# Four small edits to a decoder layer: weight sums on VectorE in one group, ScalarE's copy before VectorE's sum, two orders

## The chip, the cores and the metric

One core of a Trainium2 chip runs the whole kernel. The metric is device time in microseconds, the median of several executions. The engines are TensorE (PE, with PEld for its weight loads), VectorE (DVE), ScalarE (ACT), GpSimd (POOL) and SyncE (SP), whose queue issues nearly all loads.

## What is computed

One decoder layer on 16 + 256 positions, width 2048, in float32:

```python
u = rms_norm(h, ffn1_norm_g);  h = h + 0.5 * swiglu(u, w_gate, w_up, w_down)     # first FFN, 5632 wide
u = rms_norm(h, mix_norm_g);   z = u @ w_in                                      # q, k, v, index heads, conv, two gates
y_attn = dsa_sparse_attention(q, k, v, qi, ki, wi, 64) @ w_attn_branch
y_conv = (gate_b * causal_depthwise_conv(gate_c * xc)) @ w_conv_branch
h = h + (sigmoid(ga) * y_attn + sigmoid(gc) * y_conv) @ w_out
u = rms_norm(h, ffn2_norm_g);  h = h + 0.5 * swiglu(u, w2_gate, w2_up, w2_down)  # second FFN
return h[:, 16:]
```

## The kernel before, in words

**Two numbers for one.** The matmuls run in a format with fewer bits than float32. Each weight tile and each activation is therefore split in two: ScalarE copies it into `hi` (`whi`, L215), VectorE subtracts that from the original to get `lo` (`wlo`, L216). A product takes three matmuls: hi x hi, hi x lo, lo x hi.

**One stream of weights.** `Stream` takes all weights in the order in which they are used. `load` (L167) issues the DMA of a 1 MB chunk on SP into a few rotating `raw` buffers; it waits there until the buffer's last reader is done. `split` makes whi and wlo of one piece (128 x 1024 at most) some pieces ahead of TensorE: `ahead` is 3 at first, with four buffers, and 5 with six from `widen` on, which comes before the second FFN. `next` hands one piece to TensorE; each call first splits ahead, then emits the work that was put off with `later` or `early`. That fixes the order of the instructions on every engine: the schedule is by hand, and each engine runs its queue in that order.

**Seven products for eight.** The gates and the second FFN work on 2 x 2 blocks of weights. A pair of kind C is multiplied plainly, in 8 products of 3 matmuls. The kinds S and D use 7 products (`group`), of sums of weights (`sa`, `sb`) and sums of tokens. For S, VectorE makes `sa` (L187) from the loaded chunk, then `sb` in two steps (L193, L194). For D, the DMA makes `sa`, under the name `sd`: one load on SP (L156), then an accumulating load of another part on POOL's queue (L157); the raw chunk holds the other three parts. `add_up` keeps up to three `sd` buffers ahead: two pairs are issued in `widen`, the others as earlier pairs are split. VectorE makes `sb` in both kinds, ahead of the split of the piece before the pair.

**Sums of tokens** (`sums_of_tokens`) are made per pair of features: ScalarE scales two tiles, VectorE makes three differences and sums (L617 to L619), and the result is split (L421, L422). The last argument of the function, `at`, puts it off by that many pieces.

**The output projection.** For the 16 tiles `po[d]`, the first six get 12 of their 16 blocks early and the last four later; the others run one after the other, in two pieces of 8 blocks. A bank holds the product with hi in its first and that with lo in its second half of columns. `add_to` (L411) adds both to h; `next_act2` and `square` follow a piece later and prepare the next norm.

**The second FFN.** Eleven groups of 512 features (`up_group`), then the down projection over 4, 4 and 3 of them (`down_group`), each in two halves. In group 0, `hook` puts the norm's matmuls (L1265) and the transposes of h (L1275, copied to `ht` by L1276) between the pairs. The norm's matmuls need the sum `ssq` (L1283), a VectorE step put off by one piece. After the last pair of kind D or S, `recombine` (L669 to L674) makes four tiles from the seven products' banks; `after_seven` and `after_end` add them to the result.

Of the kernel before, what the change touches and what calls it, by code (L numbers as in the profile page):

```python
# [9 lines left out]
F32 = mybir.dt.float32  # L10
F32R = mybir.dt.float32r
AF = mybir.ActivationFunctionType
ALU = mybir.AluOpType
AX = mybir.AxisListType

P = 128
# [35 lines left out]
WIDE = 512  # L52
NG = FF // WIDE
PAIRS = KD // 2
KINDS = "DCDCDCCC"
ORDER = [3, 0, 5, 1, 7, 2, 4, 6]
# [7 lines left out]


def pairs_up(g):
    return list(zip("CCCDCDCC", range(PAIRS)) if g == 0 else zip(KINDS, ORDER))


def pairs_gate(c):  # L70
# [3 lines left out]
def pairs_down(gs, half):  # L74
    a = list(gs)
    if len(a) > 3:
        kinds, at = [
            ("CCDCDCDC", [(0, 2), (1, 2), (0, 0), (2, 2), (1, 0), (3, 0), (2, 0), (3, 2)]),
            ("CDCDCDCC", [(0, 2), (0, 0), (1, 2), (1, 0), (2, 2), (2, 0), (3, 0), (3, 2)]),
        ][half]  # L80
    else:
        kinds, at = [
            ("CCDCDC", [(0, 2), (1, 2), (0, 0), (2, 0), (1, 0), (2, 2)]),
            ("CDDCCC", [(0, 2), (0, 0), (1, 0), (1, 2), (2, 0), (2, 2)]),
        ][half]
    return [(k, a[i], f) for k, (i, f) in zip(kinds, at)]

# [8 lines left out]
class Stream:  # L96
# [7 lines left out]
    def __init__(self, nc, raw_pool, split_pool):  # L104
        self.nc = nc
        self.raw_pools, self.raw_bufs, self.n_raw = [raw_pool], RAW_BUFS, 0
        self.split_pools, self.ahead, self.n_tiles = [split_pool], AHEAD, 0
        self.sum_pool = None
        self.loads, self.subs = [], []
        self.raw, self.ready, self.sums, self.summed = {}, {}, {}, set()  # L110
        self.n_loaded = self.n_split = self.at = 0
        self.blocks, self.waiting, self.steps = [], [], []
        self.first = []
        self.added, self.doubles, self.n_added = {}, [], 0
# [56 lines left out]
    def sum_ahead(self):  # L171

        add = self.nc.vector.tensor_add
        for g, kind, _, _, _ in self.subs[self.n_split : self.n_split + 2]:
            if kind == "sa" and self.sum_pool and g not in self.summed:
                self.load(g + self.raw_bufs)
                self.summed.add(g)
                raw = self.raw[g]
                sb = self.sum_pool.tile([P, 2 * WIDE], F32, name="sb", tag="sb")
                if g in self.added:  # L180
                    sa, one, last = self.sums[g, "sa"], raw[:, :WIDE], raw[:, 2 * WIDE : 3 * WIDE]
                else:
                    sa, one, last = (
                        self.sum_pool.tile([P, 2 * WIDE], F32, name="sa", tag="sa"),
                        raw[:, WIDE : 2 * WIDE], raw[:, 3 * WIDE :],
                    )
                    add(  # L187
                        sa.rearrange("p (q c) -> p q c", q=2),
                        raw[:, WIDE : 3 * WIDE].rearrange("p (q c) -> p q c", q=2),
                        raw[:, :WIDE].rearrange("p (q c) -> p q c", q=1).to_broadcast([P, 2, WIDE]),  # L190
                    )
                    self.sums[g, "sa"] = sa
                add(sb[:, :WIDE], sa[:, WIDE:], one)  # L193
                add(sb[:, WIDE:], sb[:, :WIDE], last)  # L194
                self.sums[g, "sb"] = sb
# [75 lines left out]
def tile_decoder_layer(  # L271
# [22 lines left out]
    nc = tc.nc  # L294
# [10 lines left out]
    st = Stream(nc, raw_pool, split_pool)  # L305
# [105 lines left out]
    def add_to(x, ps, scale, pairs):  # L411

        n = x.shape[1]
        nc.vector.scalar_tensor_tensor(x, ps[:, :n], scale, x, op0=ALU.mult, op1=ALU.add)
        if pairs:
            u = tmp.tile([P, T], F32, name="u", tag="sq")[:, :SEQ]
            nc.scalar.activation(u, ps[:, SEQ:], AF.Copy, scale=scale)
            nc.vector.tensor_add(x, x, u)

    def split_into(hi, lo, src):  # L420
# [200 lines left out]
    def sums_of_tokens(i, gain, to, at=0):  # L621

        x = small_tile("m0").rearrange("p (j t) -> p j t", j=2)
        t = small_tile("m1")

        def scaled(j):
            d = 2 * i + j
            nc.scalar.activation(x[:, j, :], h[:, d, META:], AF.Copy, scale=gain[:, d : d + 1])

        st.later(lambda: [scaled(j) for j in range(2)], at + 1)  # L630
        st.later(lambda: sums_into(t, x), at + 2)
        st.later(lambda: split_into(to[:, 0, :], to[:, 1, :], t), at + 3)
# [15 lines left out]

            st.later(after)

    def group(todo, hook, after_seven, after_end):

        kinds = [k for k, _, _ in todo]
        nc_ = kinds.count("C")
        ns = len(kinds) - nc_
        last = max(n for n, k in enumerate(kinds) if k != "C")
        q = {}

        def of(tag):
            if tag not in q:  # L660
                q[tag] = [bank(tag, tag), 0, {"q2": ns + 2 * nc_, "q3": ns + 2 * nc_, "q4": ns + 2 * nc_, "q8": 2 * nc_}.get(tag, ns)]
            return q[tag]

        buf = {}

        def recombine():
            a, v, x, e = (small_tile(n) for n in "avxe")
            buf.update(q2=a, q3=v, q4=x, q8=e)
            nc.scalar.activation(a, q["q1"][0], AF.Copy)  # L669
            st.later(lambda: nc.vector.tensor_sub(v, q["q6"][0], a), 1)  # L670
            st.later(lambda: nc.vector.tensor_add(x, q["q7"][0], v), 2)
            st.later(lambda: nc.vector.tensor_sub(v, q["q5"][0], v), 3)
            st.later(
                lambda: nc.vector.scalar_tensor_tensor(e, q["q5"][0], -1.0, x, op0=ALU.mult, op1=ALU.add), 4  # L674
            )
            if after_seven:
                for i, tag in enumerate(buf):
                    st.later(lambda tag=tag: after_seven(tag, buf[tag]), 5 + i // 2)

        for n, (kind, four, ts) in enumerate(todo):  # L680
            b11, b12, b21, b22 = four()
            if kind != "C":
                t1, t3, t2, t4 = (both(ts()[:, :, f * P : (f + 1) * P]) for f in range(4))
                for tag, t in (
                    ("q7", t3), ("q5", t1), ("q6", t2), ("q3", b22), ("q1", b11), ("q4", t4), ("q2", b21)
                ):
                    mac3(of(tag), t, st.next())
                if n == last:
                    st.early(recombine)
            else:  # L690
                plain_half(b11, b12, b21, b22, of("q2"), of("q3"))
                if n == len(todo) - 1:
                    st.early(lambda: after_end(q, buf, ("q2", "q3")))
                hook(n)
                plain_half(b11, b12, b21, b22, of("q4"), of("q8"))
        st.early(lambda: after_end(q, buf, ("q4", "q8")))

    with ExitStack() as mix:
# [37 lines left out]
        steps = st.steps  # L736
# [388 lines left out]

        act1 = act[:, :, :, LATER + META : LATER + T]
        made1 = {i: gp.tile([P, 2, 4 * P], F32R, name=f"made{i}") for i in SEVEN}
        for n, (i, to) in enumerate(made1.items()):
            sums_of_tokens(i, gains[1], to, 3 * n)

        ms, merged = {}, []
        places = [[("tA", 4)], [("tB", 4)], [("zz0", 2), ("zz1", 2)], [("c0", 4)]]
# [92 lines left out]
    room[0] = left  # L1225

    ht = [left.tile([P, D], F32, name=f"ht{j}") for j in range(NT)]
    more = left.tile([P, 3, 2, 4 * P], F32R, name="more")
    third = left.tile([P, 2, 4 * P], F32R, name="third")
    made_of(SEVEN[2], 12)  # L1230
# [89 lines left out]
    def down_group(gs, final):  # L1320
        for half in range(2):
            pairs = pairs_down(gs, half)

            def place(tag, half=half):
                j, c = PLACES[tag]
                c = half * 2 * WIDE + c * WIDE
                return j, c, ht[j][:, c : c + WIDE]

            met = dict.fromkeys(PLACES, 0)

            def add_half(tag, x, place=place, met=met):
                j, c, to = place(tag)
                nc.vector.scalar_tensor_tensor(to, x, 0.5, to, op0=ALU.mult, op1=ALU.add)
                met[tag] += 1
                if final and met[tag] == 2:
                    nc.sync.dma_start(out[j * P : (j + 1) * P, c : c + WIDE], to)

            def after_end(q, buf, tags, add_half=add_half):
                for tag in tags:
                    add_half(tag, q[tag][0])  # L1340

            group(
                [
                    (k, lambda g=g, f=f: four_of(mids[g], f, f + 1), lambda g=g, f=f: made_mid[g, f])
                    for k, g, f in pairs
                ],
                lambda n: n == 1 and half == 0 and turn_mid(("q6", "q1")), add_half, after_end,
            )

    right = []  # L1350
# [155 lines left out]
```

## Time and profile before

| | |
|---|---|
| median of 3 runs | 2152.8 us (2152.34 to 2153.24) |
| the profiled execution | 2151.74 us, its span 2150.0 us |
| busy | PE 2127.5 us (99%), DVE 1500.8 (70%), ACT 1081.8 (50%), POOL 82.3 (4%) |
| granted TensorE clock over the span | 0.999 |
| loads of kind D's sums | 48 on SP and 48 on POOL, 512 KB each |

Times in rows are microseconds from the start of the span. A row of a timeline gives start, duration, engine, line, operation, output<-inputs, and in brackets the idle time just before it with what ended it. L12 is line 12 of the kernel. Rows of waits read: engine, tile and line that waited, for whom, us in total, times, longest. The span ends with the output's DMAs; between the span and the execution's time lie 1.74 us.

### The profile page before, as it was taken

How to read it: one execution, taken by the hardware profiler on the slowest of the kernel's cores; microseconds unless marked ns; L12 is line 12 of the kernel's file. 1: busy time of each engine (PE TensorE's matmuls, PEld its weight loads, DVE VectorE, ACT ScalarE, POOL GpSimd, SP SyncE). 2: the span in 40 equal slices, each digit the busy share in tenths (PEclk: the TensorE clock that was granted, in tenths of full speed). 3: DMA queues.
4: the chain of work that ended last, by engine and by line, in shares of the span. 5: the costliest groups of instructions: out<-in, count | busy, mean ns of one | idle time of the engine just before them, and what ended most of it. 6: DMA issues, size and time to landing. Idle time of an engine off the chain costs nothing.

```text
span 2150.0 us, 32021 instructions
## 1 busy us (share of the span) xinstructions
PE 2127.5 (99%) x13045; PEld 1917.2 (89%) x13045; DVE 1500.8 (70%) x1919; ACT 1081.8 (50%) x1398; POOL 82.3 (4%) x94
## 2 busy tenths in 40 slices
PE   8999999999999999999999999999999999999999
PEld 8999999999999998889988888887888888888887
DVE  7555544455555556687578777678888988888887
ACT  6444433344444445465455555466555555555553
POOL 2000000000000000000000000010000000000000
PEclk9999999999999999999999999999999999999999
DMA  6555555555555555444555556469887887788773
GB/s 242 196 177 177 177 177 177 179 178 178 181 180 181 179 177 177 157 156 139 176 180 199 178 188 214 158 219 277 260 270 220 258 278 250 249 246 284 241 245 128
DMA packets 70996, 435.47 MB, mean 203 GB/s; under 512 B 7904, under 2 KB 8032, under 8 KB 30272
## 3 DMA queue, kind: packets, MB, share of 16 engines
q1 hardware_dynamic: 63648, 407.66, 53.6%
q0 software_dynamic: 7056, 25.59, 6.8%
q8 instruction: 102, 1.67, 0.3%
q14 instruction: 46, 0.38, 0.0%
q10 hardware_dynamic: 144, 0.17, 0.0%
HBM read 431.29 MB, written 2.10 MB: 202 GB/s over the span
## 4 chain that ended last, share of the span: by engine, by line
PE 92%; DVE 4%; ACT 1%; DMA 1%; issue 1%; POOL 1%; SPq 0%; ACTq 0%; POOLq 0%
PE q L593 13%; PE q L592 13%; PE q L594 13%; PE pd L388 4%; PE pd L386 4%; PE pd L387 4%; PE pg L387 4%; PE pu L387 4%; PE pg L388 4%; PE pu L388 4%; PE pg L386 4%; PE pu L386 4%; DVE wlo L216 2%; PE pbr L592 1%; PE pbr L594 1%; PE pbr L593 1%
## 5 line engine op out<-in xcount | busy, mean ns | idle before, releaser
L216 DVE TENSOR_TENSOR wlo<-raw,whi 128x1024 fp32r<-128x1024 f32 (+1 forms) x753 | 878.0, 1173 | 586.2 <-ACT whi L215 572.1
L215 ACT ACTIVATE whi<-raw 128x1024 fp32r<-128x1024 f32 (+1 forms) x753 | 760.2, 1016 | 876.1 <-PE q L594 219.2
L592 PE MATMUL q<-whi,act 128*128 128x512 f32 x833 | 325.7, 391 | 0.0
L593 PE MATMUL q<-wlo,act 128*128 128x512 f32 x833 | 324.7, 390 | 0.8 <-DVE wlo L216 0.8
L594 PE MATMUL q<-whi,act 128*128 128x512 f32 x833 | 324.3, 389 | 0.0
L386 PE MATMUL pd<-mid,whi 128*128 128x272 f32 x704 | 201.7, 286 | 0.0
L387 PE MATMUL pd<-mid,whi 128*128 128x272 f32 x704 | 201.7, 286 | 0.0
L388 PE MATMUL pd<-mid,wlo 128*128 128x272 f32 x704 | 201.7, 286 | 0.0
L386 PE MATMUL pg<-act,whi 128*128 128x272 f32 x672 | 192.7, 287 | 0.0
L387 PE MATMUL pg<-act,whi 128*128 128x272 f32 x672 | 192.5, 287 | 0.0
L388 PE MATMUL pg<-act,wlo 128*128 128x272 f32 x672 | 192.5, 287 | 0.0
L386 PE MATMUL pu<-act,whi 128*128 128x272 f32 x672 | 192.5, 286 | 0.0
L387 PE MATMUL pu<-act,whi 128*128 128x272 f32 x672 | 192.5, 286 | 0.0
L388 PE MATMUL pu<-act,wlo 128*128 128x272 f32 x672 | 192.5, 286 | 0.0
L593 PEld LDWEIGHTS q<-wlo,act 128*128 128x128 f32 x833 | 156.6, 188 | 33.6 <-DVE wlo L216 1.9
L594 PEld LDWEIGHTS q<-whi,act 128*128 128x128 f32 x833 | 156.5, 188 | 32.5
L592 PEld LDWEIGHTS q<-whi,act 128*128 128x128 f32 x833 | 156.7, 188 | 32.1
L386 PEld LDWEIGHTS pd<-mid,whi 128*128 128x128 f32 x704 | 132.6, 188 | 0.0
L387 PEld LDWEIGHTS pd<-mid,whi 128*128 128x128 f32 x704 | 132.6, 188 | 0.0
L388 PEld LDWEIGHTS pd<-mid,wlo 128*128 128x128 f32 x704 | 132.6, 188 | 0.0
L388 PEld LDWEIGHTS pg<-act,wlo 128*128 128x128 f32 x672 | 126.6, 188 | 0.0
L386 PEld LDWEIGHTS pg<-act,whi 128*128 128x128 f32 x672 | 126.6, 188 | 0.0
(288 smaller groups left out, 3787.0 us busy)
## 6 DMA issues: line engine op xcount, KB each, us to landing
raw<-in_wgu_dram SPq DMA_DIRECT2D x87, 1024.0 KB, 4.8
raw<-in_w_dram SPq DMA_DIRECT2D x84, 1024.0 KB, 6.0
raw<-in_wd_dram SPq DMA_DIRECT2D x44, 1024.0 KB, 4.7
raw<-in_w2d_dram SPq DMA_DIRECT2D x48, 768.0 KB, 6.3
raw<-in_wg_dram SPq DMA_DIRECT2D x32, 1024.0 KB, 4.8
raw<-in_wcv_dram SPq DMA_DIRECT2D x24, 1024.0 KB, 4.8
sd<-in_w2d_dram SPq DMA_DIRECT2D x48, 512.0 KB, 6.0
sd<-in_w2d_dram POOLq DMA_DIRECT2D x48, 512.0 KB, 7.7
```

The source lines that it names most:

```text
L215: nc.scalar.activation(to[0], raw, AF.Copy)
L216: nc.vector.tensor_sub(to[1], raw, to[0].bitcast(F32))
L386: nc.tensor.matmul(ps, whi, xhi, start=first, stop=False)
L387: nc.tensor.matmul(ps, whi, xlo, start=False, stop=False)
L388: nc.tensor.matmul(ps, wlo, xhi, start=False, stop=last)
L592: nc.tensor.matmul(ps, xhi, whi, start=n == 0, stop=False)
L593: nc.tensor.matmul(ps, xhi, wlo, start=False, stop=False)
L594: nc.tensor.matmul(ps, xlo, whi, start=False, stop=n == total - 1)
```

## The change

Four edits. In group 0 of the second FFN's up projection the pairs 3 and 5 are of kind S instead of D; the tile for their `sa` is lent by the second half of `ht[1]`. In `add_to`, ScalarE's copy of the second half is issued ahead of VectorE's sum. In the second half of the last down projection the kinds run C D C D C C instead of C D D C C C, and its recombination runs at once instead of spread over several pieces. In the gates, the third sums of tokens are put off by 16 pieces instead of 6.

```diff
 def pairs_up(g):
-    return list(zip("CCCDCDCC", range(PAIRS)) if g == 0 else zip(KINDS, ORDER))
+    return list(zip("CCCSCSCC", range(PAIRS)) if g == 0 else zip(KINDS, ORDER))
...
-            ("CDDCCC", [(0, 2), (0, 0), (1, 0), (1, 2), (2, 0), (2, 2)]),
+            ("CDCDCC", [(0, 2), (0, 0), (1, 2), (1, 0), (2, 0), (2, 2)]),
...
-        self.sum_pool = None
+        self.sum_pool = self.lent = None
...
-                        self.sum_pool.tile([P, 2 * WIDE], F32, name="sa", tag="sa"),
+                        self.lent if self.lent is not None else self.sum_pool.tile([P, 2 * WIDE], F32, name="sa", tag="sa"),
...
     def add_to(x, ps, scale, pairs):
         n = x.shape[1]
-        nc.vector.scalar_tensor_tensor(x, ps[:, :n], scale, x, op0=ALU.mult, op1=ALU.add)
         if pairs:
             u = tmp.tile([P, T], F32, name="u", tag="sq")[:, :SEQ]
             nc.scalar.activation(u, ps[:, SEQ:], AF.Copy, scale=scale)
+        nc.vector.scalar_tensor_tensor(x, ps[:, :n], scale, x, op0=ALU.mult, op1=ALU.add)
+        if pairs:
             nc.vector.tensor_add(x, x, u)
...
-    def group(todo, hook, after_seven, after_end):
+    def group(todo, hook, after_seven, after_end, spread=True):
...
+            for i, fn in enumerate(steps):           # steps: the four VectorE steps of recombine
+                st.later(fn, 1 + i if spread else 1)
             if after_seven:
                 for i, tag in enumerate(buf):
-                    st.later(lambda tag=tag: after_seven(tag, buf[tag]), 5 + i // 2)
+                    st.later(lambda tag=tag: after_seven(tag, buf[tag]), 5 + i // 2 if spread else 2)
...
-        for n, (i, to) in enumerate(made1.items()):
-            sums_of_tokens(i, gains[1], to, 3 * n)
+        for at, (i, to) in zip((0, 3, 16), made1.items()):
+            sums_of_tokens(i, gains[1], to, at)
...
     ht = [left.tile([P, D], F32, name=f"ht{j}") for j in range(NT)]
+    st.lent = ht[1][:, 2 * WIDE :]
...
                 lambda n: n == 1 and half == 0 and turn_mid(("q6", "q1")), add_half, after_end,
+                not (final and half == 1),
```

More of the change, by code (lines that the diff above doesn't have):

```diff
@@ L669, in recombine @@
             nc.scalar.activation(a, q["q1"][0], AF.Copy)
[L670 to L675, printed above, removed]
+            steps = [
+                lambda: nc.vector.tensor_sub(v, q["q6"][0], a),
+                lambda: nc.vector.tensor_add(x, q["q7"][0], v),
+                lambda: nc.vector.tensor_sub(v, q["q5"][0], v),
+                lambda: nc.vector.scalar_tensor_tensor(e, q["q5"][0], -1.0, x, op0=ALU.mult, op1=ALU.add),
+            ]
+            for i, fn in enumerate(steps):
+                st.later(fn, 1 + i if spread else 1)
             if after_seven:
                 for i, tag in enumerate(buf):
-                    st.later(lambda tag=tag: after_seven(tag, buf[tag]), 5 + i // 2)
+                    st.later(lambda tag=tag: after_seven(tag, buf[tag]), 5 + i // 2 if spread else 2)
         for n, (kind, four, ts) in enumerate(todo):
```

## The prediction

> **What bounds the kernel now.** I read the busy shares first, then TensorE's waits, then the chain of waits, then the timeline around each wait. TensorE is busy 99% of the span, so only its idle places can be won. Its waits over the whole run name them (engine, tile and line, for whom, us in total, times, longest):
>
> ```profile
> PE norm L1265 <- DVE ssq L1283: 4.3, 1, 4.3
> PE po L401 <- ACT whi L215: 2.7, 4, 0.8
> ...
> PE q L592 <- DVE ve L674: 1.1, 1, 1.1
> ```
>
> The longest stands early in the second FFN's group 0. The chain of waits (start, us, what) says what it waits for:
>
> ```profile
> 1439.86 5.13 DMA sd<-in_w2d_dram
> 1445.06 0.51 issue
> 1445.57 8.08 DMA sd<-in_w2d_dram
> 1453.68 0.70 DVE sb L193
> 1454.40 0.69 DVE sb L194
> 1455.09 2.27 DVE wlo L216 x2
> 1457.76 0.89 PE norm L1265 x4
> 1458.64 1.81 PE pht L1275 x8
> 1486.82 1.44 PE pht L1275 x12
> ```
>
> Two DMAs one after the other (a load, then an accumulating load on POOL's queue) make the first weight sum. VectorE stands before it with `sb`, and the small add `ssq` (L1283), which the norm's matmuls need, is queued behind. The windows show more (stretch, us, then busy time and count of PE, PEld, DVE, ACT, POOL, granted clock, DMA share, GB/s):
>
> ```profile
> 1457.80:1461.40 3.60, 3.60 (x15) 3.41 (x16) 3.60 (x4) 3.58 (x5) 0.00 (x0) 0.53 0.92 375
> 1461.40:1486.40 25.00, 25.00 (x111) 20.66 (x111) 19.61 (x29) 15.40 (x21) 2.62 (x3) 1.00 1.00 294
> ```
>
> After the stop TensorE runs at a granted clock of 0.53 for some 3.6 us, then at full clock with 25.00 / 111 = 0.225 us per matmul (0.227 is the spacing of the starts below). So I price a stop by start times, not by idle time:
>
> ```profile
> 1453.06 0.39 PE L594 MATMUL q<-whi,act 128*128 128x512 f32 x1
> ...
> 1461.45 0.39 PE L592 MATMUL q<-whi,act 128*128 128x512 f32 x1
> ```
>
> Between these starts lie 8.39 us. At full clock I expect 4 matmuls of 512 columns (0.91), 8 transposes (1.44 x 8/12 = 0.96) and the 4 norm matmuls (their 0.89 at half clock, so an estimate of 0.4): 2.27. The stop costs 6.1 us. [...]
>
> The second place is the start of the one-by-one output tiles of the output projection, in TensorE's timeline:
>
> ```profile
> 1378.63 2.04 PE L401 MATMUL po<-ms,whi 128*128 128x512 f32 x8
> ...
> 1396.41 2.00 PE L401 MATMUL po<-ms,whi 128*128 128x512 f32 x8
> ```
>
> Five half tiles (8 blocks each) take 17.78 us. Unhindered:
>
> ```profile
> 1396.40:1438.30 41.90, 41.90 (x242) 36.88 (x241) 33.50 (x53) 26.74 (x46) 4.03 (x4) 1.00 0.58 201
> ```
>
> 15 half tiles in 41.90 us, 2.79 each. So this place loses 17.78 - 13.97 = 3.8 us.
>
> **The change part by part.**
>
> *ScalarE's copy first.* At a tile's end VectorE multiplies one half of the bank into h (L414), ScalarE copies the other half (L417), VectorE adds it (L418). On each engine the order stays; what turns is who waits, as the waits of this stage show:
>
> ```profile
> ACT u L417 <- DVE h L414: 27.1, 16, 2.0
> ...
> DVE h L418 <- ACT u L417: 8.0, 16, 0.5
> ```
>
> All 16 tiles: ScalarE stands 1.7 us, with the next weight split (whi, L215) queued behind the copy, and VectorE 0.5 us; then VectorE stands again for that whi. With the copy first, ScalarE needs only the matmuls, done several us earlier, and copies while VectorE is still in its previous wlo. VectorE then runs L414 and L418 back to back. It saves 8.0 us of standing on VectorE over 16 tiles, and about as much again behind whi. Followed step by step at the place of the loss, each whi is then ready about 1 us before TensorE needs it. Bounds: 0, if the wait turns without getting shorter, to 3.8. I take 3.6, near the upper end, because VectorE is busy only 33.50 of 41.90 us even in the crowded part. From there on the stage is bound by TensorE. [...]
>
> *Group 0 with weight sums on VectorE.* Two pairs change from D to S. Removed per pair: a 512 KB load on SP, an accumulating 512 KB load on POOL, and 768 KB of raw; added: 1024 KB of raw on SP, in the same place of its queue, and one 128x1024 sum on VectorE. Traffic falls by 2 x 768 KB. The sum's row stands in the gates' first group, in the chain:
>
> ```profile
> 1105.38 1.23 DVE wlo L216
> 1107.60 1.15 DVE sa L187
> ```
>
> 2 x 1.15 = 2.3 us more on VectorE. The first lies where VectorE stands waiting for the DMA until 1453.68, the second in group 0 behind TensorE's pace, so both cost nothing; without that cover they would cost 2.3. VectorE's last work before it stood still:
>
> ```profile
> 1446.45 2.36 DVE L216 TENSOR_TENSOR wlo<-raw,whi 128x1024 fp32r<-128x1024 f32 x2 [0.44 <-ACT whi L215]
> ```
>
> With nothing but this change VectorE would begin the sum there, at 1448.8, and do sum, sb, sb, wlo, wlo, ssq (1.15 + 0.70 + 0.69 + 2.27 + 0.4, the last from 1457.36 to 1457.76): 1454.0 against 1453.3, when TensorE is ready. That leaves 0.8 idle and saves 5.3. With the faster output projection VectorE is some 4 us earlier relative to TensorE, and the stop goes: 6.1. Next in line is then the raw load of the second S pair. Its predecessor, 768 KB, took:
>
> ```profile
> raw<-in_w2d_dram SPq DMA_DIRECT2D x1, 768.0 KB, 9.8
> ```
>
> By size that is 13.1 us for 1024 KB. By the order of the queues its sum is wanted some 13 us after its issue, and TensorE can wait for it about 5 us more (both estimates from the paces above): hidden. The sum's tile is the half of ht[1] that the transposes fill only at the group's end; the second sum reuses it after the first's two reads, long done. The sd buffers are loaded as early as before, now for group 1; the third pair there has its load issued only when the first is split (last rival).
>
> *Third token sums later.* Their three VectorE steps fill the gap between the two rows above (1106.61 to 1107.60, 1.0 us), ahead of the second S pair's sum, which holds up the next wlo. TensorE there:
>
> ```profile
> 1110.19 0.39 PE L592 MATMUL q<-whi,act 128*128 128x512 f32 x1
> 1111.37 0.50 PE L593 MATMUL q<-wlo,act 128*128 128x512 f32 x1 [0.80 <-DVE wlo L216]
> 1111.71 0.40 PE L594 MATMUL q<-whi,act 128*128 128x512 f32 x1
> 1111.94 0.40 PE L592 MATMUL q<-whi,act 128*128 128x512 f32 x1
> ```
>
> 1.75 us for three matmuls instead of 0.68: 1.07 lost. Taking 1.0 us out ahead of it brings the wlo to its time with 0.1 to spare; I take 1.0 (0.8 to 1.07). The sums now stand ten blocks later, among plain pairs, where TensorE needs 12 x 0.227 = 2.7 us per split and VectorE about 1.2 plus one or two steps of 0.7; their 1.0 and the 0.7 of their split fit. They are first used in the next column of gates.
>
> *Order of the last half.* C D D C C C becomes C D C D C C. The second D's two sb steps stand today ahead of the step `ve`, which frees the bank that the first D's second matmul group writes:
>
> ```profile
> 2116.18 0.61 DVE sb L193
> 2116.81 0.69 DVE sb L194
> ```
>
> ```profile
> 2118.57 0.39 PE L592 MATMUL q<-whi,more 128*128 128x512 f32 x1
> ...
> 2121.30 0.39 PE L592 MATMUL q<-whi,more 128*128 128x512 f32 x1
> ```
>
> 2.73 us for six matmuls instead of 1.36: 1.37 lost. The sb steps (1.3) move behind `ve`, so I take 1.3 (0.9 to 1.37). In exchange the last recombination has two C pairs left (2 x 24 x 0.227 = 10.9 us) instead of three. It is 8 VectorE steps of about 0.65 and a copy of 0.6, 5.8 in all, and the change lets them run at once: hidden, and the tail behind the last matmul stays. If VectorE came to them over 5 us late, they would cost up to 5.
>
> **Sum.** 3.6 + 6.1 + 1.0 + 1.3 = 12.0 us. The profiled execution took 2151.74 (span 2150.0, 1.74 around it), 1.06 below the median. So 2139.7 for it, and 2152.8 - 12.0 = 2140.8 for the median.
>
> **The rivals.**
>
> *The wait turns and stays.* VectorE stands 0.5 us for the copy at each tile as now. Against it: ScalarE waits 1.7 us there for nothing else, so it can be early. The 3.8 stay and 0.8 of the norm's stop: 5.3 + 1.0 + 1.3 = 7.6 to 7.7, time 2145.1. Chance 0.08.
>
> *The raw loads bound the start of the one-by-one tiles.* The tiles before them are small and quickly used up, so three loads of 1024 KB come close together. If half the 3.8 stays: 2142.6. Chance 0.12.
>
> *A new wait in group 0*, on the second S pair's raw or on the lent tile. A stop of 4 us in place of 6.1, so 8.0 saved in all: 2144.8. Chance 0.08.
>
> *Slower: the third pair of group 1.* Its load and accumulation are issued when the group's first pair is split. Needed one D (21 matmuls), one C (24), one D and half a C later, 78 x 0.227 = 17.7 us, and VectorE leads TensorE there by some 4.6 us (an estimate from the same pace): 22.3. The slowest of this region:
>
> ```profile
> sd<-in_w2d_dram SPq DMA_DIRECT2D x1, 512.0 KB, 7.9
> sd<-in_w2d_dram POOLq DMA_DIRECT2D x1, 512.0 KB, 10.7
> ```
>
> With the 0.5 of issue between them, as in the chain, 19.1, so it is hidden by 3. It becomes slower than before from 22.3 + 12.0 = 34.3 us on; at 37 it would be 2155.5. Chance 0.03.
>
> **How the numbers follow.** The forecast has 0.67, with an own range of 2139.6 to 2142.0; a further 0.02 is for no change at all. The range 2139.6 to 2145.3 takes in the three rivals that are also faster. Faster by over 0.2% (4.3 us, about what a measurement of this kernel can tell): 0.94; the rest 0.03 and 0.03.
>
> **What would show it.** Right: no wait of TensorE for ssq, none for whi at the first one-by-one tiles, none at the gates' second S pair or at the last half's first D; ScalarE no longer waits for L414, VectorE's L414 hardly for the copy; clock 1.00 throughout group 0; 46 sd loads. Wrong: VectorE idle ahead of L414 in every tile; a wait for raw or sd in groups 0 and 1; VectorE still recombining at the last matmul.

## The result, and the profile after

The changed kernel takes 2140.69 us (median of 6 runs, 2140.57 to 2141.47); the kernel before, run beside it, 2152.66 (6 runs, 2152.18 to 2153.66). The ratio is 0.9945, its 95% interval 0.9932 to 0.9957. The forecast was 2140.8.

The profiled execution took 2141.47 us, its span is 2139.7. The busy shares and the loads of kind D's sums (groups of DMA issues: count, KB each, median us from issue to landing):

```profile
PE 2124.4 (99%) x13045; PEld 1915.1 (90%) x13045; DVE 1502.4 (70%) x1921; ACT 1083.5 (51%) x1398; POOL 79.2 (4%) x92
...
sd<-in_w2d_dram POOLq DMA_DIRECT2D x46, 512.0 KB, 8.2
```

TensorE executes as many matmuls as before. VectorE has two instructions more, POOL two fewer. The shares hardly differ; what has gone is in TensorE's waits over the whole run (engine, tile and line, for whom, us in total, times, longest):

```profile
PE start L386 <- ACT whi L215: 7.3, 2, 6.8
...
PE pbr L593 <- DVE ve L675: 0.4, 1, 0.4
```

The four waits that the prediction went for (norm on `ssq`, po on `whi`, q on `ve`, q on `wlo`) are gone. Behind the start of the run one is new: `pbr`, the product of the attention and convolution branches, waits for `ve`.

The sum of what went is best seen between TensorE's first and last matmul, first in the kernel before, then in the changed one (timeline):

```profile
6.01 0.59 PE L386 MATMUL start<-act,whi 128*128 128x272 f32 x1 [6.01 <-ACT whi L215]
...
2145.57 0.39 PE L594 MATMUL q<-whi,mid 128*128 128x512 f32 x1
```

```profile
6.76 0.60 PE L386 MATMUL start<-act,whi 128*128 128x272 f32 x1 [6.76 <-ACT whi L215]
...
2134.80 0.39 PE L595 MATMUL q<-whi,mid 128*128 128x512 f32 x1
```

2139.56 us has become 2128.04: 11.5 us less. The two profiled executions differ by 2151.74 - 2141.47 = 10.3 only. Of the rest, 0.75 us lie at the start, where the first weights came later in the second, and 0.5 us behind the last matmul: from its start to the end of the span it is 4.4 us before and 4.9 after, and 4.9 too in experiments 2 and 3, which leave the last half alone.

**The output projection** (timeline of TensorE; the same five half tiles as in the prediction):

```profile
1379.11 2.11 PE L401 MATMUL po<-ms,whi 128*128 128x512 f32 x8
...
1393.18 1.09 PE L401 MATMUL po<-ms,whi 128*128 128x512 f32 x4
```

14.07 us instead of 17.78, at TensorE's own pace of 2.79 per half tile. The waits of the same stage:

```profile
ACT whi L215 <- DMA raw<-in_wo_dram: 3.6, 2, 3.0
...
ACT u L416 <- PE po L403: 2.0, 1, 2.0
DVE h L417 <- ACT u L416: 1.0, 1, 1.0
```

ScalarE's copy (now L416) no longer waits for VectorE; VectorE's sum (now L417) waits for the copy once in 16 tiles, 1.0 us in all, where the pair of waits came to 27.1 and 8.0. TensorE bounds the stage. (The 3.0 us that ScalarE stood for a raw load at its start held TensorE up by 0.1.)

**Group 0 of the second FFN** (TensorE's timeline, then VectorE's, then a window with busy time and count of PE, PEld, DVE, ACT, POOL, granted clock, DMA share, GB/s):

```profile
1449.83 0.39 PE L595 MATMUL q<-whi,act 128*128 128x512 f32 x1
...
1452.03 0.39 PE L593 MATMUL q<-whi,act 128*128 128x512 f32 x1
```

```profile
1440.76 1.22 DVE L187 TENSOR_TENSOR ht<-raw 128x1024 f32<-128x1024 f32 x1
...
1445.62 0.41 DVE L1287 TENSOR_TENSOR ssq<-ssq,ssq 128x256 f32<-128x256 f32 x1
```

```profile
1450.00:1475.00 25.00, 25.00 (x118) 20.88 (x118) 19.81 (x28) 17.35 (x22) 0.00 (x0) 1.00 0.57 202
```

The step that took 8.39 us takes 1452.03 - 1449.83 = 2.20. The weight sum (`ht<-raw`, in the lent tile) costs 1.22 us of VectorE, and `ssq` is done 4 us before TensorE asks for it. The granted clock is 1.00 in the whole window.

**The gates.** The second S pair runs through. The matmul at which TensorE now stops is the branch product, 18 us later (timelines of TensorE and of VectorE):

```profile
1110.92 0.39 PE L593 MATMUL q<-whi,act 128*128 128x512 f32 x1
...
1111.71 0.39 PE L593 MATMUL q<-whi,act 128*128 128x512 f32 x1
...
1129.40 0.39 PE L593 MATMUL pbr<-whi,ys 128*128 128x512 f32 x1
...
1130.66 0.50 PE L593 MATMUL pbr<-whi,ys 128*128 128x512 f32 x1 [0.43 <-DVE ve L675]
```

```profile
1123.67 0.42 DVE L618 TENSOR_TENSOR vm<-vm 128x256 f32<-128x256 f32 x1
...
1129.93 0.68 DVE L675 SCALAR_TENSOR_TENSOR ve<-q,vx 128x512 f32<-128x512 f32 x1
```

The three matmuls at 1110.92 take 0.79 instead of 1.75. But the third sums of tokens (L618 to L620) and half of their split (L423) now stand in VectorE's queue ahead of the last steps of a recombination. Its `ve` is late, and the bank that it reads is the one into which the second branch product goes: 1130.66 - 1129.40 = 1.26 for three matmuls.

**The last half** (TensorE, then VectorE):

```profile
2109.10 0.39 PE L593 MATMUL q<-whi,more 128*128 128x512 f32 x1
...
2110.51 0.40 PE L593 MATMUL q<-whi,more 128*128 128x512 f32 x1
```

```profile
2108.98 0.68 DVE L675 SCALAR_TENSOR_TENSOR ve<-q,vx 128x512 f32<-128x512 f32 x1
...
2128.99 0.68 DVE L1337 SCALAR_TENSOR_TENSOR ht<-ve,ht 128x512 f32<-128x512 f32 x1
```

1.41 us for six matmuls instead of 2.73: `ve` now stands ahead of `sb`. The last of the recombined adds (`ht<-ve`) begins 6 us before the last matmul, so none of them stands behind it: in both kernels VectorE's last work ends 1.1 us after the last matmul's start.

By their places the four edits give 3.7 + 6.2 + 0.4 + 1.3 = 11.6 us, within 0.1 of what went between first and last matmul. The 0.4 is 1.75 - 0.79 = 0.96, less the new stop: 1.26 against 0.69 where that product isn't held up (experiment 6), 0.57.

### The profile page after: what moved, and what is told of

Same layout as the page of the kernel before. It is cut to its first block, busy times and chain, and to the rows that moved or that the text cites. A ratio compares the mean times of both kernels' runs of the same rounds, so it can differ in the third digit from the quotient of the medians.

```text
span 2139.7 us, 32014 instructions
## 1 busy us (share of the span) xinstructions
PE 2124.4 (99%) x13045; PEld 1915.1 (90%) x13045; DVE 1502.4 (70%) x1921; ACT 1083.5 (51%) x1398; POOL 79.2 (4%) x92
## 4 chain that ended last, share of the span: by engine, by line
PE 97%; DVE 1%; ACT 1%; DMA 1%; POOL 0%; issue 0%; SPq 0%; DVEq 0%
PE q L594 13%; PE q L593 13%; PE q L595 13%; PE pd L386 4%; PE pd L388 4%; PE pd L387 4%; PE pu L388 4%; PE pg L388 4%; PE pg L387 4%; PE pu L387 4%; PE pg L386 4%; PE pu L386 4%; PE po L401 3%; PE po L403 1%; PE pbr L593 1%; PE pbr L594 1%
## 5 line engine op out<-in xcount | busy, mean ns | idle before, releaser
L386 PEld LDWEIGHTS pg<-act,whi 128*128 128x128 f32 x672 | 126.6, 188 | 0.0
L387 PEld LDWEIGHTS pg<-act,whi 128*128 128x128 f32 x672 | 126.6, 188 | 0.0
```

The source lines that it names most:

```text
L386: nc.tensor.matmul(ps, whi, xhi, start=first, stop=False)
L387: nc.tensor.matmul(ps, whi, xlo, start=False, stop=False)
```

## The experiments

The theory: the four terms of the prediction add up, each where it said. The rival views to be told apart: that one of the first two edits does the other's work as well, by VectorE's lead or by the shorter way to the first weight sum; that an order brings nothing, or needs its neighbour edit. Experiments 1 to 4 ran on one chip (kernel before: 2151.59 in the median, 2150.39 to 2154.17), 5 to 8 on another (2151.9, 2149.6 to 2154.28).

**1. The kernel before with only ScalarE's copy first.**

```diff
     def add_to(x, ps, scale, pairs):
-        nc.vector.scalar_tensor_tensor(x, ps[:, :n], scale, x, op0=ALU.mult, op1=ALU.add)
         if pairs: ... copy on ScalarE ...
+        nc.vector.scalar_tensor_tensor(x, ps[:, :n], scale, x, op0=ALU.mult, op1=ALU.add)
```

> The kernel before with ScalarE's copy first in add_to, nothing else. Theory: the loss at the first one-by-one tiles (3.8 us) goes, but the norm's stop has a cause of its own, the load and the accumulating load of sd, which are issued only when the output projection ends. [...] So 3.6 + 6.1 - 2.3 = 7.4 us faster: 2145.3. Rival A: VectorE's lateness was the cause of both, and the copy alone removes both: 9.7 us, 2143.0. Rival B: the stop stays as long and the clock halves as before: 3.6 us, 2149.1.

Measured: 2144.75 (8 runs, 2143.91 to 2147.55), ratio 0.997 (0.996 to 0.9981). A row of TensorE's waits, its timeline at the norm, and two windows there:

```profile
PE po L401 <- ACT whi L215: 0.3, 1, 0.3
```

```profile
1450.63 0.39 PE L595 MATMUL q<-whi,act 128*128 128x512 f32 x1
1453.51 0.61 PE L1266 MATMUL norm<-ones,ssq 128*128 128x2 f32 x4 [2.48 <-DVE ssq L1284]
...
1456.82 0.63 PE L593 MATMUL q<-whi,act 128*128 128x512 f32 x1
```

```profile
1451.02:1454.10 3.08, 0.60 (x6) 0.59 (x6) 3.08 (x4) 3.08 (x5) 0.00 (x0) 1.00 0.38 82
1454.20:1457.50 3.30, 3.30 (x13) 2.92 (x12) 3.30 (x6) 2.95 (x4) 0.00 (x0) 0.50 1.00 412
```

The po wait is 0.3 instead of 2.7: this part of the edit needs no other. The norm's stop is shorter but there: 6.19 us from 1450.63 to 1456.82, against 2.20 in the changed kernel, so it costs 4.0 us. The idle time of 2.48 us is near the 2.3 in the expected sum, the author's estimate from the lengths in the chain of waits before. The sum counts that stop at full clock, which no run had shown, and this was wrong: the granted clock is 1.00 while TensorE stands and 0.50 from about 1454.2 to 1457.5.

By the medians the edit brings 6.8 of the 7.4 us expected. The profiled execution took 2147.48, near the upper end of the eight. Its trace has a second stretch at half clock, from 17.3 to 20.5 us, which the profiled execution of the kernel before doesn't have (1.00 there); the granted clock over the span is 0.998, before 0.999. The four executions with a granted clock of 1.000 over the span took 2143.91 to 2144.42. Some 3.4 us at half clock (0.53 over 1454 to 1457 and 0.90 over 1457 to 1460) take 0.0008 off the mean of the span, so these four can hardly have had such a stretch. That the clock halves at this stop in some executions of one kernel and not in others is therefore likely, by an estimate from these means, but they left no trace that shows it. The rival that the copy alone removes the norm's stop falls, at least for the execution that was seen.

**2. The kernel before with only group 0's pairs of kind S.**

```diff
-    return list(zip("CCCDCDCC", range(PAIRS)) if g == 0 else zip(KINDS, ORDER))
+    return list(zip("CCCSCSCC", range(PAIRS)) if g == 0 else zip(KINDS, ORDER))
...
+    st.lent = ht[1][:, 2 * WIDE :]
```

> The kernel before with kind S for the two pairs of group 0 (and the lent tile), nothing else. Theory: the loss at the first one-by-one tiles stays at 3.8 us with ScalarE waiting 27 us for L414; the norm's stop shrinks from 4.3 to about 0.8 us of idleness at full clock: 5.3 us faster, 2147.4. Rival: the sums' 2.3 us on a VectorE that is late anyway take the place of the DMA's wait, and the stop stays above 3 us: under 2 us faster, over 2150.7.

Measured: 2147.8 (11 runs, 2147.18 to 2149.14), ratio 0.9982 (0.9974 to 0.9991). A row of TensorE's waits, its timeline, and a window:

```profile
PE q L592 <- ACT ht L1277: 0.3, 1, 0.3
```

```profile
1453.46 0.39 PE L594 MATMUL q<-whi,act 128*128 128x512 f32 x1
1454.44 0.61 PE L1266 MATMUL norm<-ones,ssq 128*128 128x2 f32 x4 [0.59 <-DVE ssq L1284]
...
1456.52 0.39 PE L592 MATMUL q<-whi,act 128*128 128x512 f32 x1
```

```profile
1455.00:1458.00 3.00, 3.00 (x19) 2.62 (x19) 3.00 (x4) 2.98 (x4) 0.00 (x0) 1.00 1.05 292
```

3.06 us for the step that takes 2.20 without a stop: 0.86 is left, near the 0.8 that the prediction gave for this edit alone, and the granted clock stays at 1.00. A wait for ScalarE's copy of the transposes (`ht`) is new: 0.3 us of idle time, 0.5 by the starts (from 1459.03 to 1459.73 for one matmul). So the trace gives 8.39 - 3.06 - 0.5 = 4.8 us of the 5.3 expected; the medians give 3.8, beside a kernel before whose runs scatter over 3.8. The rival (under 2 us) falls. The S pairs remove nearly all of the stop by themselves. What is left comes from VectorE's lateness behind the output projection: with the copy first (experiment 3) it is gone.

**3. Both of them.**

> The kernel before with both of these edits and without the other two. Theory: the two add up to 9.7 us, as the prediction had it (3.6 + 6.1): 2143.0; from the trace of the changed kernel the other two edits are worth 1.3 + 0.35, which gives 2142.4. Rival: the edits overlap, so that together they bring no more than the better one alone: 2145 or more.

Measured: 2143.09 (5 runs, 2142.32 to 2143.2), ratio 0.996 (0.9946 to 0.9973). Besides the waits at the start of the run TensorE keeps those that the two orders are for:

```profile
PE q L593 <- DVE ve L675: 1.1, 1, 1.1
...
PE q L594 <- DVE wlo L216: 0.8, 1, 0.8
```

The waits of po and norm are gone. TensorE's timeline at their places, the five half tiles and the step at the norm:

```profile
1379.45 2.12 PE L401 MATMUL po<-ms,whi 128*128 128x512 f32 x8
...
1393.53 2.00 PE L401 MATMUL po<-ms,whi 128*128 128x512 f32 x8
...
1450.18 0.39 PE L595 MATMUL q<-whi,act 128*128 128x512 f32 x1
...
1452.38 0.39 PE L593 MATMUL q<-whi,act 128*128 128x512 f32 x1
```

14.08 us instead of 17.78 and 2.20 instead of 8.39: 3.7 + 6.2 = 9.9 us, where the prediction's first two terms make 9.7. The medians show 8.5 us beside a kernel before that scatters over 3.8, so the terms are better read from the trace. The rival (2145 or more) falls. The stop at the norm goes completely only with both edits: each by itself leaves a part of it, 2.5 or 0.6 us of idle time.

**4. The changed kernel with its last recombination spread as before.** Only the argument `not (final and half == 1)` is taken out.

> The changed kernel with the last recombination spread over several pieces again (the order C D C D C C kept). Theory: with two C pairs left instead of three the four adds of the recombined tiles come behind the last matmul: 4 x 0.6 = 2.4 us slower than the changed kernel, 2143.1. Rival: there is room enough either way, and the time stays at 2140.7.

Measured: 2143.76 (5 runs, 2143.51 to 2145.12), ratio 0.9965 (0.9953 to 0.9978). The end of VectorE's timeline; TensorE's last matmul starts at 2135.38:

```profile
2138.22 0.69 DVE L1337 SCALAR_TENSOR_TENSOR ht<-ve,ht 128x512 f32<-128x512 f32 x1
```

Put off piece by piece, the four adds of recombined tiles come due when no piece is left, and stand behind the last matmul. VectorE ends 3.5 us after that matmul's start instead of 1.1: the 2.4 expected. With the output's DMAs behind them the stretch to the end of the span is 7.9 us instead of 4.9, and the median lies 3.1 above the changed kernel's (2140.69). The order C D C D C C is worth its 1.3 only together with the recombination at once; by itself it would lose more than it wins (it was not run without the other edits).

**5. The changed kernel again**, beside the three below.

> The changed kernel again, for comparison with the next three on the same chip. All theories: 2140.7.

Measured: 2141.17 (5 runs, 2140.72 to 2141.82), ratio 0.9948 (0.9934 to 0.9962). One of TensorE's waits differs from the first profile:

```profile
PE po L401 <- ACT whi L215: 0.7, 1, 0.7
```

It stands at the first one-by-one tile. ScalarE stood there for 3.02 us in the first profile (for a raw load, hidden but for 0.1) and for 3.73 here; this time the trace names TensorE as the releaser. But it was the load again. The one that `whi` needs was issued on SP at 1371.35 (DMA issues):

```profile
raw<-in_wo_dram SPq DMA_DIRECT2D x1, 1024.0 KB, 6.9
```

So it landed at 1378.3, and `whi` starts at 1378.37. In the first profile it landed at 1377.9 (1371.69 + 6.2), and `whi` started at 1378.00.

**6. The changed kernel with the third token sums at 6 pieces again.**

```diff
-        for at, (i, to) in zip((0, 3, 16), made1.items()):
+        for at, (i, to) in zip((0, 3, 6), made1.items()):
```

> The changed kernel with the third sums of tokens back at 6 pieces. The trace of the changed kernel shows 0.96 us won at the second S pair of the gates' first group, but a new wait of TensorE, for the recombination's last step, at the start of the branch products (0.6 us more than before there). Theory from the trace: 0.35 us slower than the changed kernel, 2141.0. The prediction's step: 1.0 us slower, 2141.7. Rival: no difference to be seen in the times; then the starts in the trace decide.

Measured: 2141.8 (5 runs, 2140.97 to 2142.12), ratio 0.9951 (0.9939 to 0.9964). TensorE at both places:

```profile
1110.67 0.39 PE L593 MATMUL q<-whi,act 128*128 128x512 f32 x1
1112.42 0.40 PE L593 MATMUL q<-whi,act 128*128 128x512 f32 x1
...
1130.13 0.39 PE L593 MATMUL pbr<-whi,ys 128*128 128x512 f32 x1
...
1130.82 0.48 PE L593 MATMUL pbr<-whi,ys 128*128 128x512 f32 x1
```

The old stop is back (1.75) and the new one is gone (0.69 instead of 1.26). So the new stop comes from this edit. The times of experiments 5 and 6 overlap and can't size it; the starts do, 0.4.

**7. The changed kernel with the last half as before**, order and recombination.

```diff
-            ("CDCDCC", [(0, 2), (0, 0), (1, 2), (1, 0), (2, 0), (2, 2)]),
+            ("CDDCCC", [(0, 2), (0, 0), (1, 0), (1, 2), (2, 0), (2, 2)]),
...
-                not (final and half == 1),
```

> The changed kernel with the last half's order and its recombination as before. Theory: the stop of 1.37 us at the first D's second group returns, nothing else: 1.3 us slower than the changed kernel, 2142.0. Rival: the gain came from the recombination at once (shorter tail), and the stop moves without costing: below 0.5 us.

Measured: 2142.22 (5 runs, 2142.11 to 2143.21), ratio 0.9955 (0.9942 to 0.9967). TensorE's timeline:

```profile
2109.50 0.39 PE L593 MATMUL q<-whi,more 128*128 128x512 f32 x1
...
2111.46 0.50 PE L593 MATMUL q<-whi,more 128*128 128x512 f32 x1 [1.12 <-DVE ve L675]
...
2112.27 0.39 PE L593 MATMUL q<-whi,more 128*128 128x512 f32 x1
```

2.77 us instead of 1.41, and a median 1.05 above experiment 5 with no overlap of the runs. The stop that the edit was for is back, 1.36 us by the starts, and the rival (below 0.5) falls.

**8. The changed kernel with the third token sums put off by 22 pieces**, past the recombination.

```diff
-        for at, (i, to) in zip((0, 3, 16), made1.items()):
+        for at, (i, to) in zip((0, 3, 22), made1.items()):
```

> The changed kernel with the third sums of tokens put off by 22 pieces, into the branch products, where VectorE has 1 to 1.5 us free per piece, instead of 16, where they stand ahead of the recombination. Theory: the gain of 0.96 us at the second S pair stays, and the wait at the branch products' start falls back to before's 0.1: 0.6 us faster than the changed kernel, 2140.1. Rival: the sums then delay the products' sigmoids or merge, and a wait shows up later in the gates: no gain.

Measured: 2140.52 (5 runs, 2139.89 to 2141.5), ratio 0.9946 (0.9934 to 0.9959). TensorE at the branch product, and VectorE where the sums now stand:

```profile
1128.97 0.39 PE L593 MATMUL pbr<-whi,ys 128*128 128x512 f32 x1
...
1129.65 0.48 PE L593 MATMUL pbr<-whi,ys 128*128 128x512 f32 x1
```

```profile
1139.73 0.42 DVE L618 TENSOR_TENSOR vm<-vm 128x256 f32<-128x256 f32 x1
```

Both stops are gone: 0.68 for the three matmuls here, and no wait of TensorE at the second S pair. The sums stand among plain pairs where VectorE waits before its splits anyway (1.32 us before the one ahead of the sums). In the trace this is worth 0.6 us more than the changed kernel; the medians differ by 0.65, but their runs overlap, so no time here proves it. It has the lowest median of all versions that were run.

## Why the prediction was right, and where not

**The whole.** Forecast 12.0 us, medians 12.0, by places 11.6. None of the rivals as a whole took place. By places the first two terms and the last came out within 0.1 us each, and the third 0.6 smaller than forecast. That the medians meet the forecast to the tenth all the same is luck: runs of the kernel before scatter over 3.8 us (experiments 1 to 4).

**The copy first: right.** 3.7 for the term of 3.6. The wait did not turn and stay: VectorE waits for the copy once, where the rival needed 16 times, and 8.0 us became 1.0, because the copy is done by the time VectorE comes. The second rival, raw loads, shows as a remnant: 0.1 us in the first profile, 0.3, 0.7 and 0.5 in experiments 1, 5 and 7 and none in the others with the copy first, where the rival needed half of 3.8. So this term is about 3.0 to 3.7 us, depending on when the load lands.

**Group 0: right in size, with the clock behind a shorter stop taken for granted.** 6.2 for 6.1, and 0.86 left without the copy for the forecast 0.8; the 0.5 for `ht` that came with it was not foreseen. The 6.2 belong to two edits, which overlap here: the copy alone takes 2.2 us off this stop (experiment 1), the S pairs alone 5.3 (experiment 2). That the two sums on VectorE are covered held too: there is no wait of TensorE for the second S pair's raw, none for the lent tile, none in group 1, whose third `sd` was there in time. Its load's issue on SP and VectorE's first use (timeline):

```profile
1472.41 1.68 SPq L156 DMA_DIRECT2D sd<-in_w2d_dram  x2
```

```profile
1491.58 0.68 DVE L193 TENSOR_TENSOR sb<-sd,raw 128x512 f32<-128x512 f32 x1
```

19.2 us lie between (the prediction had 22.3), and `sb` did not wait: the accumulating load, issued at 1478.43, landed 8.2 us later, at 1486.6, with 5 us to spare. What failed is full clock behind a shorter stop, which the 7.4 of experiment 1 counts on and no run had shown: there the granted clock fell to 0.50 behind 2.48 us of idle time. The prediction's 5.3, for 0.8 us of idle time, counts on it too, and at 0.59 us (experiment 2) the clock did stay at 1.00; between the two nothing was run. The sum of 12.0 didn't hang on it, since the stop went altogether.

**The third token sums: the step that was mis-sized.** Forecast 1.0, measured 0.4. The stop that it aimed at went as said (0.96). But the step "their 1.0 and the 0.7 of their split fit" compared VectorE's mean load with TensorE's pace. It did not look at the recombination that stands at the same place, whose last step has a due time: it frees a bank. The late step costs 0.57 us there. Experiments 6 and 8 show that the new stop comes and goes with the place of these sums alone.

**The last half's order: right.** 1.3 forecast; 1.32 by the starts before and after, 1.05 by the medians of experiments 5 and 7. The cover that was named for the recombination, two C pairs, held; experiment 4 shows the price when the steps are spread past it: 2.4 us of VectorE behind the last matmul, 2.6 by the medians of experiments 4 and 5 (on two chips).

## What to carry to other kernels

Price a stop of the bounding engine from the start of the matmul before it to that of one well behind it, against the same stretch unhindered: idle time alone left out a third of this one (4.3 of 6.2 us). Where two engines read one bank in turn, as ScalarE and VectorE do here, issue first the one that has other work queued behind, if the other comes late anyway: here ScalarE's 27.1 us of waiting for VectorE went, and VectorE's 8.0 for the copy became 1.0. When a step is put off, look in the new place for the next step behind it that frees a buffer, not only for room on the engine: here the late `ve` cost 0.57 us.

## What the hardware showed that was not expected

The granted clock fell from 1.00 to 0.50 at a stop of 2.48 us of idle time (experiment 1). It did not fall while TensorE stood: in experiment 1 it is 1.00 up to 1454.1, through the four matmuls of two columns, and falls during the transposes, some 3.2 us after the end of the last matmul of 512 columns (1450.63 + 0.39). Then it is 0.50 for some 3.4 us (estimated from the two means in experiment 1); the 0.53 of the prediction's window is a mean that takes in a little of full clock. In the kernel before it is 1.00 through 4.3 us of idle time too and falls to 0.50 at about 1457.9, as work begins; it is back at 1.00 at 1461.4. Whether the fall belongs to the gap or to the small matmuls behind it was not tried. The slow part costs what the idle row doesn't show: 6.19 - 2.20 = 4.0 us by the starts for 2.5 of idleness, as before 6.2 for 4.3.
